# A hybrid encoder block on one core: the order of its first loads, of work at four seams, and of the last rows

## The chip, the cores and the metric

The kernel runs on one core of a Trainium2 chip. Its time is the device time of one execution in microseconds (us). Five engines work beside each other, each in the order of its own instruction list: PE (TensorE, matmuls and transposes), DVE (VectorE), ACT (ScalarE), POOL (GpSimd) and SP (SyncE, which here only issues DMAs). ACT and POOL can issue DMAs too. An instruction waits on semaphores for what it reads, and holds up what stands behind it on its engine.

## What is computed

x has 1024 rows of 1024 columns, fp32. Cut to what matters:

```
h      = rmsnorm(x) ; u = h @ w_in          # z, xbc, dt, s_b, s_c, s_x, g_a, g_b
y      = scan(silu(conv(xbc)), dt) * silu(z) # chunked state-space scan, 4 groups
y      = y * rsqrt(mean(y*y over a group)) * ssd_norm_w
branch_a = y @ w_ssd_proj
branch_b = (s_b * conv(s_c * s_x)) @ w_sconv_proj
x      = x + (sigmoid(g_a) * branch_a + sigmoid(g_b) * branch_b) @ w_o
f      = rmsnorm(x)
x      = x + (silu(f @ w_gate) * (f @ w_up)) @ w_down
out    = rmsnorm(x)
```

## The kernel before

**Matmuls.** Every large product is a Strassen-Winograd product of 2x2 blocks: seven block products in the order 1, 2, 6, 5, 7, 3, 4, on operands such as A11, S1 to S4 and B11, T1 to T4, which are sums of blocks. Each fp32 operand is split into a hi and a lo part (ACT writes hi: th, wh, wk, gh, qh; DVE subtracts for lo: tl, wl, wk, gl, ql), and each product of two tiles is three matmuls (`mmc`, L678 to L681: hi hi, lo hi, hi lo). A matmul of 128x512 starts some 0.23 us behind the one before it.

**Order.** The program is written out by hand: each engine runs its instructions in the order of the code. Generators (`put`, `step_norms`, `h1_rows`) are stepped from the loops of matmuls, so that a step's place in the loops is its place on DVE, ACT and POOL. Pages of 4 KB a partition are taken from a pool of 47 and go back when their readers are through.

**Prologue.** x lies in eight tiles of 128 rows (x0 to x7). SP issues x0 to x3 (L231), the first weight tile p0.y (`first[0].y.load()`, tile ws), x4 to x7 (`more_loads`, L245), p1.y and p2.y, the small weights of dt (wdts, L1501), and the three p.x. POOL issues six small loads of constants into c (L236 to L241), then d, dtbc and al. Rows 0 to 3 are squared by ACT, DVE, ACT, DVE (`rows_sq(..., "avav")`, L115 and L117). PE transposes the constants into pc (L1532, L1533), ACT copies them to cols (L1534). Then ACT's square root nr (L101) and four small DVE operations (L102 to L107) give the factors of the rows, rows are scaled (L135 on ACT, L137 on DVE), turned by PE (L1543), copied with the norm's weight (br), and split into th and tl.

**T2 seam.** `second_half` turns rows 4 to 7; a pass k of its loop writes one quarter of the raw blocks and of the sums t1 and t2 (L1602). `put("T1")` splits t1 in pass 3; `put("T2")` splits t2 behind the loop, one yield later. wk and u are parts of the weight operands and of the products' sums beside it.

**Norm seam.** The scan's output y is normed per group and half of the rows: gv, gr (L99 to L107) from the sums of squares pq, PE turns gr into prt (L532), ACT copies it to rst, POOL writes it to rs_d in memory (L536) and reads it back spread over all partitions (rbc, L538), DVE multiplies y by it (L543). When the second half of a group is done, its sums for the next product are made (L557) and written to yt_d (L558). Several norms run at once; `step_norms` steps them oldest first.

**h1 seam.** Before the FFN, the rows of the first half are scaled by their norm in `h1_rows(0, (2, 3))`: rows 2 and 3 on ACT (L135), the others on DVE (L137), turned, and split (gh, qh on ACT; gl, ql on DVE).

**Tail.** For each of the last four row tiles `fin` adds the two sums of squares (fss, L1423), takes the root (fr, L1411) and four small DVE operations, scales one half of the row on ACT (L1486) and one on DVE (L1428), and SP writes the row out (L1488).

Of the kernel before, what the change touches and what calls it, by code (L numbers as in the profile page):

```python
# [8 lines left out]
F32 = mybir.dt.float32  # L9
# [4 lines left out]
P = 128  # L14
# [25 lines left out]
def hybrid_block(ctx: ExitStack, tc: tile.TileContext, x, nmw, w_in, cw, cb, dtb, alog, dsk, snw,  # L40
# [15 lines left out]
    def nm(s):  # L56
        cnt[0] += 1
        return f"{s}_{cnt[0]}"
# [4 lines left out]
    def bank(s):  # L63
        return sm.tile([P, 512], F32, tag="sm", name=nm(s))
# [58 lines left out]
    def rows_sq(src, s, engs="aaaa"):  # L123
        acc = rows_acc(src, s)
        for e in engs:
            rows_sq_on(e, acc, s)
        return acc
# [29 lines left out]
    class Slab:  # L157
# [1 line left out]
            self.src, self.shape, self.s = src, shape, s  # L159
            self.st = self.hl = None  # L160

        def load(self):
            if self.st is None:
                self.st = page(self.s + "s", self.shape)
                nc.sync.dma_start(self.st, self.src)

        def split(self):
            if self.hl is None:
# [57 lines left out]
    xt = [page("x") for _ in range(NT)]  # L226
    wdt_s = sp.tile([P, KT * H], F32, tag="eb", bufs=3, name="wdts").rearrange("p (k h) -> p k h", h=H)
    warm = cp.tile([P, 1], F32, name="warm")
    nc.scalar.activation(warm, epst, AF.Sqrt)
    for i in range(4):  # L230
        nc.sync.dma_start(xt[i], x[i * P:(i + 1) * P, :])  # L231


    consts = page("c")
# [5 lines left out]
    nc.gpsimd.dma_start(rb[40:56, :], snw.rearrange("o (i p) -> (o i) p", p=P))  # L240
    nc.gpsimd.dma_start(rb[56:80, :], scw[0].rearrange("k (i p) -> (k i) p", p=P))  # L241

    def more_loads():
        for i in range(4, NT):
            nc.sync.dma_start(xt[i], x[i * P:(i + 1) * P, :])  # L245
    d2 = cp.tile([16, 2], F32, name="d2")

    dtbc = cp.tile([H, 1], F32, name="dtbc")
# [2 lines left out]
    def small_loads():  # L251
        nc.gpsimd.dma_start(d2, dsk.rearrange("o (i j) -> (o i) j", j=2))
        nc.gpsimd.dma_start(dtbc, dtb.rearrange("o h -> h o"))
        for q in range(4):
            nc.gpsimd.dma_start(al[32 * q:32 * q + 32, :], alog.rearrange("o h -> h o"))
# [305 lines left out]
    def scans():  # L561


        def step_norms():
            for n in list(norms):
                if next(n, 0) == 0:
                    norms.remove(n)

        def one(f, j):
            f(j)  # L570
            step_norms()

        want(0, 0)
        want(0, 2)
        prep(0)
        prep(1)
        prep_eb(1)
        yield
        prep2(0)
        for j in range(len(items)):  # L580
            one(part1, j)
            yield
            if j > 0:
                one(part2, j - 1)
                yield
        one(part2, len(items) - 1)
        yield
        while norms:
            step_norms()
            yield  # L590
# [553 lines left out]
    def h1_rows(half, act):  # L1144
        ts = range(4 * half, 4 * half + 4)
        s = sp.tile([P, 4], F32, tag="ssq", name=nm("hss"))
        V.tensor_add(s.unsqueeze(2), sq1[:, 4 * half:4 * half + 4, 0:1], sq1[:, 4 * half:4 * half + 4, 1:2])
        rows = rows_scale([h1[t] for t in ts], [hn[t] for t in ts], s, act=act)
        for t in ts:
            nc.sync.dma_start(h1_d[t], h1[t])  # L1150
            h1[t] = hn[t] = None
        return rows
# [10 lines left out]
    def ffn_phase():  # L1163
# [17 lines left out]
        raw0, raw1 = ([], []), ([], [])  # L1181

        def first_half():
            rows0 = h1_rows(0, (2, 3))
            yield
            yield
            yield from fill(rows0, raw0, 0, wcol)
            yield from put("B11", raw0[0])
            yield from put("B21", raw0[1])
# [214 lines left out]
            no = slice(j * 512, j * 512 + 512)  # L1404
            nc.scalar.activation(fo[t][:, no], h1[t][:, no], AF.Square, accum_out=sq[:, t, j:j + 1])

        def rstd2_of(ssq, n, s):

            shp = list(ssq.shape)
            r = sp.tile(shp, F32, tag="rr", name=nm(s + "r"))  # L1410
            nc.scalar.activation(r, ssq, AF.Sqrt, scale=1.0 / n, bias=epst)  # L1411
            v = sp.tile(shp, F32, tag="rv", name=nm(s + "v"))
            V.tensor_scalar(v, ssq, 1.0 / n, EPS, op0=ALU.mult, op1=ALU.add)
            V.reciprocal(r, r)
            q = sp.tile(shp, F32, tag="rq", name=nm(s + "q"))
            V.tensor_mul(q, r, r)
            V.tensor_mul(q, q, v)
            V.scalar_tensor_tensor(r, q, -3.0, r, op0=ALU.add, op1=ALU.mult)
            return r

        def finish(ms):
            s = sp.tile([P, len(ms), 1], F32, tag="fss", name=nm("fss"))
            V.tensor_add(s, sq[:, ms[0]:ms[-1] + 1, 0:1], sq[:, ms[0]:ms[-1] + 1, 1:2])  # L1423
            return rstd2_of(s.rearrange("p a b -> p (a b)"), D, "f")

        def out_rows(t, r, n):
            no = slice(n * 512, n * 512 + 512)
# [52 lines left out]
        tail = ds.chunks[ds.at:]  # L1480
        ds.ahead(len(ds.chunks), len(ds.chunks))

        def fin(m):
            t = 4 + m
            r = finish(range(t, t + 1))
            nc.scalar.activation(fo[t][:, 512:1024], h1[t][:, 512:1024], AF.Copy, scale=r)  # L1486
            out_rows(t, r, 0)
            nc.sync.dma_start(out[t * P:(t + 1) * P, :], fo[t])  # L1488

        for m in range(4):  # L1490
            for c in tail:
# [3 lines left out]


    first[0].y.load()
    more_loads()
    for p in first[1:]:
        p.y.load()  # L1500
    nc.sync.dma_start(wdt_s, w_in[:, DT0:DT0 + H].rearrange("(k p) f -> p k f", p=P))  # L1501
    for p in first:
        p.x.load()
    small_loads()
    loaded[0] = NF
    steps_ps, wdt_hl = [], []

# [17 lines left out]
            mmc(steps_ps[hf][:H], wh[:, kw, :], wl[:, kw, :], bh, bl, j == 0 and part == 0,  # L1525
                j == len(todo) - 1 and part == 1)

    a0 = rows_sq(xt[0:4], "x", "avav")
    a1 = rows_acc(xt[4:8], "x")
    del xt  # L1530
    pc = bank("pc")
    nc.tensor.transpose(pc[:, 0:96], ra, ident[:96, :96])  # L1532
    nc.tensor.transpose(pc[:, 96:176], rb, ident[:80, :80])  # L1533
    nc.scalar.activation(cols[:, 0:176], pc[:, 0:176], AF.Copy)  # L1534
    del consts, ra, rb
    r0 = rows_scale(*a0, act=(3,), parts=2)
    raw0, raw1 = ([], []), ([], [])
    turned = {}
# [53 lines left out]
    def second_half():  # L1592
        t1, t2 = [[page("t1", HB) for _ in range(2)] for _ in range(2)]
        for k in range(KT):
            if k % 2 == 0:
                raw1[k // 4].append(page("br", HB))
            turn_rows(r1, k)
            pt = turned.pop(k)
            o = k % 4 // 2, k % 2
            nc.scalar.activation(raw1[k // 4][o[0]][:, o[1], :], pt, AF.Copy, scale=nmc[:, k:k + 1])  # L1600
            less = (raw0[0] if k < 4 else t1)[o[0]][:, o[1], :]
            V.scalar_tensor_tensor((t1, t2)[k // 4][o[0]][:, o[1], :], pt, nmc[:, k:k + 1], less,  # L1602
                                   op0=ALU.mult, op1=ALU.subtract)
            if k == 3:
                raw0[0].clear()
                for j in range(2):
                    nc.sync.dma_start(b12_d[j], raw1[0][j])
                every(put("T1", t1))
            yield
        every(put("T2", t2))  # L1610
        yield
        every(put("B22", raw1[1]))
        yield
        for k in range(2):
            V.tensor_sub(raw1[0][k], raw1[1][k], raw1[0][k])
        every(put("T3", raw1[0]))
        raw1[0].clear()
        raw1[1].clear()
        yield
        for k in range(2):  # L1620
            V.tensor_sub(raw0[1][k], raw0[1][k], t2[k])
        every(put("T4", raw0[1]))
        raw0[1].clear()
        yield
# [104 lines left out]
```

## Time and profile before

| | |
|---|---|
| median of 3 runs | 1910.57 us (1910.33 to 1910.74) |
| profiled execution | 1910.68 us, its span 1908.9 us |
| PE busy | 1879.7 us, 98% of the span |
| DVE, ACT, POOL busy | 68%, 51%, 9% |
| DMA moved | 411.97 MB, mean 216 GB/s |
| chain that ended last | PE 92%, DVE 4%, ACT 2%, DMA 1%, issue 1% |

The span goes from the first to the last instruction of the profile. In rows of the timeline, the idle time ahead of an instruction and what ended it stand in brackets; idle time of PE is what a change here can give back.

### The profile page before, as it was taken

How to read it: one execution, taken by the hardware profiler on the slowest of the kernel's cores; microseconds unless marked ns; L12 is line 12 of the kernel's file. 1: busy time of each engine (PE TensorE's matmuls, PEld its weight loads, DVE VectorE, ACT ScalarE, POOL GpSimd, SP SyncE). 2: the span in 40 equal slices, each digit the busy share in tenths (PEclk: the TensorE clock that was granted, in tenths of full speed). 3: DMA queues.
4: the chain of work that ended last, by engine and by line, in shares of the span. 5: the costliest groups of instructions: out<-in, count | busy, mean ns of one | idle time of the engine just before them, and what ended most of it. 6: DMA issues, size and time to landing. Idle time of an engine off the chain costs nothing.

```text
span 1908.9 us, 24143 instructions
## 1 busy us (share of the span) xinstructions
PE 1879.7 (98%) x8905; PEld 1545.3 (81%) x8905; DVE 1299.4 (68%) x1688; ACT 970.6 (51%) x1541; POOL 169.7 (9%) x196
## 2 busy tenths in 40 slices
PE   7999999999999999999999999999999999999998
PEld 5688888888888888888878888887888888888886
DVE  7667878777785678889878548877444444456465
ACT  5545454444444987877665454464333333345333
POOL 1010111101100000101010000101211121100000
PEclk9999999999999999999999999999999999999999
DMA  5197999978959656778798665917988888867552
GB/s 181 48 275 173 240 230 236 240 187 226 264 149 288 223 194 219 251 250 269 261 321 311 226 208 203 229 80 171 215 193 220 195 193 192 232 257 286 190 196 110
DMA packets 341190, 411.97 MB, mean 216 GB/s; under 512 B 17384, under 2 KB 223936, under 8 KB 341072
## 3 DMA queue, kind: packets, MB, share of 16 engines
q1 hardware_dynamic: 284400, 308.59, 50.0%
q0 software_dynamic: 48608, 72.47, 20.9%
q10 hardware_dynamic: 8064, 29.36, 3.8%
q8 instruction: 70, 1.15, 0.2%
q14 instruction: 48, 0.39, 0.1%
HBM read 320.56 MB, written 143.15 MB: 243 GB/s over the span
## 4 chain that ended last, share of the span: by engine, by line
PE 92%; DVE 4%; ACT 2%; DMA 1%; issue 1%; SPq 0%; ACTq 0%; DVEq 0%
PE pb L679 5%; PE pb L680 5%; PE pb L681 5%; PE gb L679 5%; PE gb L680 5%; PE gb L681 5%; PE fb L681 4%; PE fb L679 4%; PE fb L680 4%; PE pr L81 4%; PE pr L83 4%; PE pr L82 4%; PE gd L679 4%; PE pd L679 4%; PE gd L681 4%; PE gd L680 4%
## 5 line engine op out<-in xcount | busy, mean ns | idle before, releaser
L77 DVE TENSOR_TENSOR wl<-ws,wh 128x1024 fp32r<-128x1024 f32 x77 | 94.0, 1221 | 121.6 <-ACT wh L76 121.6
L679 PE MATMUL gb<-qh,gh 128*128 128x512 f32 x432 | 169.1, 391 | 1.1 <-DVE h L1132 1.1
L680 PE MATMUL gb<-ql,gh 128*128 128x512 f32 x432 | 168.9, 391 | 0.0
L681 PE MATMUL gb<-qh,gl 128*128 128x512 f32 x432 | 168.7, 391 | 0.0
L681 PE MATMUL fb<-th,wl 128*128 128x512 f32 x352 | 137.1, 389 | 0.8 <-DVE wl L77 0.8
L679 PE MATMUL fb<-th,wh 128*128 128x512 f32 x352 | 137.1, 390 | 0.6 <-ACT wh L76 0.6
L680 PE MATMUL fb<-tl,wh 128*128 128x512 f32 x352 | 137.0, 389 | 0.0
L81 PE MATMUL pr<-th,wh 128*128 128x512 f32 x320 | 131.1, 410 | 0.0
L679 PE MATMUL gd<-qh,gh 128*128 128x512 f32 x324 | 126.0, 389 | 0.0
L680 PE MATMUL gd<-ql,gh 128*128 128x512 f32 x324 | 126.0, 389 | 0.0
L681 PE MATMUL gd<-qh,gl 128*128 128x512 f32 x324 | 126.0, 389 | 0.0
L83 PE MATMUL pr<-th,wl 128*128 128x512 f32 x320 | 125.1, 391 | 0.0
L82 PE MATMUL pr<-tl,wh 128*128 128x512 f32 x320 | 124.9, 390 | 0.0
L76 ACT ACTIVATE qh<-cb 128x1024 fp32r<-128x1024 f32 x98 | 99.8, 1018 | 38.0 <-PE gb L680 17.1
L77 DVE TENSOR_TENSOR ql<-cb,qh 128x1024 fp32r<-128x1024 f32 x98 | 115.6, 1180 | 1.6 <-ACT qh L76 1.4
L74 DVE SCALAR_TENSOR_TENSOR gl<-ca,gh 128x1024 fp32r<-128x1024 f32 (+1 forms) x60 | 70.5, 1174 | 49.0 <-ACT gh L73 49.0
L681 PE MATMUL fd<-th,wl 128*128 128x512 f32 x264 | 102.7, 389 | 0.0
L679 PE MATMUL fd<-th,wh 128*128 128x512 f32 x264 | 102.7, 389 | 0.0
L680 PE MATMUL fd<-tl,wh 128*128 128x512 f32 x264 | 102.7, 389 | 0.0
L679 PEld LDWEIGHTS gb<-qh,gh 128*128 128x128 f32 x432 | 81.5, 189 | 18.4 <-DVE h L1132 1.4
L679 PE MATMUL pb<-th,wh 128*128 128x512 f32 x240 | 94.4, 394 | 1.0 <-ACT u L894 1.0
L681 PEld LDWEIGHTS gb<-qh,gl 128*128 128x128 f32 x432 | 81.5, 189 | 17.1
(324 smaller groups left out, 4702.3 us busy)
## 6 DMA issues: line engine op xcount, KB each, us to landing
ws<-in_w_in_dram SPq DMA_DIRECT2D x80, 512.0 KB, 6.3
ws<-in_w_gate_dram SPq DMA_DIRECT2D x77, 256.0 KB, 3.9
ws<-in_w_up_dram SPq DMA_DIRECT2D x77, 256.0 KB, 4.4
ca<-u_d SPq DMA_DIRECT2D x35, 512.0 KB, 5.3
ab<-ac_d SPq DMA_DIRECT2D x32, 512.0 KB, 6.0
xbc_g<-cv ACTq DMA_DIRECT2D x24, 512.0 KB, 7.0
ws<-ws POOLq DMA_DIRECT2D x22, 512.0 KB, 6.4
wd_d<-in_w_down_dram SPq DMA_DIRECT2D x20, 512.0 KB, 10.8
```

Source lines behind the costliest of these rows:

```text
L74: nc.vector.scalar_tensor_tensor(lo, src, -1.0, hi.bitcast(F32), op0=ALU.mult, op1=ALU.subtract)
L76: nc.scalar.activation(hi, src, AF.Copy)
L77: nc.vector.tensor_sub(lo, src, hi.bitcast(F32))
L81: nc.tensor.matmul(o, lh, rh, start=first, stop=False)
L82: nc.tensor.matmul(o, lh, rl, start=False, stop=False)
L83: nc.tensor.matmul(o, ll, rh, start=False, stop=last)
L679: nc.tensor.matmul(o, lh, rh, start=first, stop=False, skip_group_check=True)
L680: nc.tensor.matmul(o, lh, rl, start=False, stop=False, skip_group_check=True)
L681: nc.tensor.matmul(o, ll, rh, start=False, stop=last, skip_group_check=True)
```

## The change

Five edits. (1) Loads of the prologue: x0 and x2 are issued by SP, x1 and x3 by ACT; SP then issues p0.y and nothing more. ACT issues x4 and x5 behind its square of x0, and x6, x7, p1.y and wdts behind its square of x2, and p2.y between cols and the root nr. POOL issues the three p.x behind the constants and ahead of d, dtbc and al. (2) `put("T2")` stands inside the last pass of the loop. (3) `step_norms` steps the newest norm first. (4) `h1_rows(0, (3,))`: row 2 is scaled by DVE. (5) In the tail the sum of squares of the first half of a row, known earlier, goes in as the bias of the root (one operation for the four rows, `known`), and the last row is written in two halves by ACT and SP.

```diff
+    for i in range(4):
+        (nc.scalar if i % 2 else nc.sync).dma_start(xt[i], x[i * P:(i + 1) * P, :])
     nc.scalar.activation(warm, epst, AF.Sqrt)
-    for i in range(4):
-        nc.sync.dma_start(xt[i], x[i * P:(i + 1) * P, :])
...
-    def more_loads():
-        for i in range(4, NT):
-            nc.sync.dma_start(xt[i], x[i * P:(i + 1) * P, :])
+    def more_loads(i):
+        for i in (i, i + 1):
+            nc.scalar.dma_start(xt[i], x[i * P:(i + 1) * P, :])
...
-            for n in list(norms):
+            for n in norms[::-1]:
...
-            rows0 = h1_rows(0, (2, 3))
+            rows0 = h1_rows(0, (3,))
...
+            r = sp.tile(shp, F32, tag="rr", name=nm("fr"))
+            nc.scalar.activation(r, ssq, AF.Sqrt, scale=1.0 / D, bias=b)
+            v = sp.tile(shp, F32, tag="fv", name=nm("fv"))
+            V.tensor_scalar(v, ssq, 1.0 / D, b, op0=ALU.mult, op1=ALU.add)
...
+        known = sp.tile([P, 4], F32, tag="rv", name=nm("fk"))
+        V.tensor_scalar(known.unsqueeze(2), sq[:, 4:8, 1:2], 1.0 / D, EPS, op0=ALU.mult, op1=ALU.add)
...
-            r = finish(range(t, t + 1))
+            r = rstd2_of(sq[:, t, 0:1], known[:, m:m + 1])
             nc.scalar.activation(fo[t][:, 512:1024], h1[t][:, 512:1024], AF.Copy, scale=r)
             out_rows(t, r, 0)
-            nc.sync.dma_start(out[t * P:(t + 1) * P, :], fo[t])
+            if m < 3:
+                nc.sync.dma_start(out[t * P:(t + 1) * P, :], fo[t])
+            else:
+                nc.scalar.dma_start(out[t * P:(t + 1) * P, 512:1024], fo[t][:, 512:1024])
+                nc.sync.dma_start(out[t * P:(t + 1) * P, 0:512], fo[t][:, 0:512])
...
-    more_loads()
-    for p in first[1:]:
-        p.y.load()
-    nc.sync.dma_start(wdt_s, w_in[:, DT0:DT0 + H].rearrange("(k p) f -> p k f", p=P))
-    for p in first:
-        p.x.load()
-    small_loads()
...
-    a0 = rows_sq(xt[0:4], "x", "avav")
+    a0 = rows_acc(xt[0:4], "x")
+    rows_sq_on("a", a0, "x")
+    more_loads(4)
+    rows_sq_on("v", a0, "x")
+    rows_sq_on("a", a0, "x")
+    more_loads(6)
+    first[1].y.load(nc.scalar)
+    nc.scalar.dma_start(wdt_s, w_in[:, DT0:DT0 + H].rearrange("(k p) f -> p k f", p=P))
+    rows_sq_on("v", a0, "x")
     a1 = rows_acc(xt[4:8], "x")
     del xt
+    for p in first:
+        p.x.load(nc.gpsimd)
+    small_loads()
...
     nc.scalar.activation(cols[:, 0:176], pc[:, 0:176], AF.Copy)
     del consts, ra, rb
+    first[2].y.load(nc.scalar)
...
-            yield
-        every(put("T2", t2))
+            if k == 7:
+                every(put("T2", t2))
+            yield
```

ACT's list at the start of the program, before (x_85 to x_88 are rows 0 to 3, ws_182 is p0.y):

```order
L229 ACT_TABLE_LOAD
L229 ACTIVATE warm<-epst 128x1
L117 ACTIVATE xn_206,xss_205<-x_85 128x1024
L117 ACTIVATE xn_210,xss_205<-x_87 128x1024
L1534 ACTIVATE cols<-pc_215 128x176
L101 ACTIVATE nr_221<-nv_219 128x4
```

The same place of the changed kernel (x_89 to x_92 are rows 4 to 7, ws_195 is p1.y, ws_217 is p2.y):

```order
L117 ACTIVATE xn_185,xss_184<-x_85 128x1024
L245 DMA x_89<-in_x_dram 128x1024
L245 DMA x_90<-in_x_dram 128x1024
L117 ACTIVATE xn_191,xss_184<-x_87 128x1024
L245 DMA x_91<-in_x_dram 128x1024
L245 DMA x_92<-in_x_dram 128x1024
L165 DMA ws_195<-in_w_in_dram 128x8x128
L1537 DMA wdts<-in_w_in_dram 128x8x32
L1547 ACTIVATE cols<-pc_213 128x176
L165 DMA ws_217<-in_w_in_dram 128x8x128
L101 ACTIVATE nr_221<-nv_219 128x4
```

Between the squares and the root nr stand seven DMA issues now, the last of them behind cols.

DVE's list at the T2 seam, before (t_72 and t_73 are the two halves of T2, s_93 and s_100 weight sums):

```order
L1602 SCALAR_TENSOR_TENSOR t_73_425<-pt_558,cols,t_71_423 128x512
L868 TENSOR_TENSOR wk_548<-s_93_546,wk_548 128x512
L847 TENSOR_TENSOR s_100_581<-ws_195,ws_188 128x512
L77 TENSOR_TENSOR tl_586<-t_72_424,th_585 128x1024
L77 TENSOR_TENSOR tl_590<-t_73_425,th_589 128x1024
L868 TENSOR_TENSOR wk_583<-s_100_581,wk_583 128x512
```

The same place of the changed kernel (s_104 is the sum that was s_100):

```order
L1616 SCALAR_TENSOR_TENSOR t_73_425<-pt_558,cols,t_71_423 128x512
L77 TENSOR_TENSOR tl_566<-t_72_424,th_565 128x1024
L77 TENSOR_TENSOR tl_570<-t_73_425,th_569 128x1024
L869 TENSOR_TENSOR wk_548<-s_93_546,wk_548 128x512
L848 TENSOR_TENSOR s_104_589<-ws_203,ws_195 128x512
```

The two tl stand ahead of the first wk and the next sum now.

DVE's list at the last norm, before (y_7211 and y_7212 are rows of the norm before it):

```order
L543 SCALAR_TENSOR_TENSOR y_7211<-y_7211,cols,rbc_8235 128x512 x2
L543 SCALAR_TENSOR_TENSOR y_7212<-y_7212,cols,rbc_8235 128x512 x2
L99 TENSOR_SCALAR gv_8383<-pq_8378 128x4
L102 RECIPROCAL gr_8385<-gr_8385 128x4
L104 TENSOR_TENSOR gq_8388<-gr_8385 128x4
L105 TENSOR_TENSOR gq_8388<-gq_8388,gv_8383 128x4
L106 TENSOR_SCALAR gq_8388<-gq_8388 128x4
L107 TENSOR_TENSOR gr_8385<-gr_8385,gq_8388 128x4
```

The same place of the changed kernel:

```order
L544 SCALAR_TENSOR_TENSOR y_7211<-y_7211,cols,rbc_8233 128x512 x2
L99 TENSOR_SCALAR gv_8380<-pq_8375 128x4
L102 RECIPROCAL gr_8382<-gr_8382 128x4
L104 TENSOR_TENSOR gq_8385<-gr_8382 128x4
L105 TENSOR_TENSOR gq_8385<-gq_8385,gv_8380 128x4
L106 TENSOR_SCALAR gq_8385<-gq_8385 128x4
L107 TENSOR_TENSOR gr_8382<-gr_8382,gq_8385 128x4
L544 SCALAR_TENSOR_TENSOR y_7212<-y_7212,cols,rbc_8233 128x512 x2
```

The whole chain from gv to gr stands ahead of the second pair of rows now. On POOL, where the order was yt_d T3, rs_d, rbc, yt_d T4, it is rs_d, rbc, yt_d T3, yt_d T4.

## Rows read from the trace of the kernel before

**Rows 1.** The page, busy time of each engine, its share and instructions:
```profile
PE 1879.7 (98%) x8905; PEld 1545.3 (81%) x8905; DVE 1299.4 (68%) x1688; ACT 970.6 (51%) x1541; POOL 169.7 (9%) x196
```

**Rows 2.** Timeline (start, length in us), prologue: ACT's, then one of DVE:
```profile
8.41 1.06 ACT L117 ACTIVATE xn<-x 128x1024 f32<-128x1024 f32 x1 [3.16 <-DMA x<-in_x_dram]
...
10.70 0.32 ACT L1534 ACTIVATE cols<-pc 128x176 f32<-128x176 f32 x1 [1.14 <-PE pc L1533]
11.41 0.20 ACT L101 ACTIVATE nr<-nv 128x4 f32<-128x4 f32 x1 [0.39 <-DVE nv L99]
...
13.90 1.04 ACT L864 ACTIVATE wh<-ws 128x1024 fp32r<-128x1024 f32 x1
...
9.86 1.23 DVE L115 SCALAR_TENSOR_TENSOR xn<-x 128x1024 f32<-128x1024 f32 x1 [3.13 <-DMA x<-in_x_dram]
```

**Rows 3.** Timeline of PE in the prologue:
```profile
10.30 0.36 PE L1533 MATMUL pc<-ident,c 80*128 80x80 f32 x1 [1.88 <-DMA c<-in_sconv_w_dram]
...
20.41 0.50 PE L680 MATMUL pb<-tl,wh 128*128 128x512 f32 x1 [0.61 <-DVE tl L77]
```

**Rows 4.** Timeline of SP's DMA issues in the prologue (the length is that of the issues):
```profile
2.60 0.44 SPq L165 DMA_DIRECT2D ws<-in_w_in_dram  x1
...
7.59 5.51 SPq L165 DMA_DIRECT2D ws<-in_w_in_dram  x2
13.15 3.15 SPq L1501 DMA_DIRECT2D wdts<-in_w_in_dram  x1
```

**Rows 5.** Issues later: ACT's, SP's (timeline); DMA view from 100.2 us (KB, us to landing):
```profile
514.41 0.33 ACTq L606 DMA_DIRECT2D xbc_g<-cv  x1
...
471.12 14.58 SPq L165 DMA_DIRECT2D ws<-in_w_in_dram  x1
...
ws<-in_w_in_dram SPq DMA_DIRECT2D x1, 512.0 KB, 16.8
```

**Rows 6.** Timeline at the T2 seam: DVE, ACT, PE:
```profile
53.19 1.41 DVE L1602 SCALAR_TENSOR_TENSOR t<-pt,cols,t 128x512 f32<-128x512 f32 x2 [1.34 <-ACT br L1600]
...
53.73 0.60 ACT L897 ACTIVATE u<-pd 128x512 f32<-128x512 f32 x1
...
57.46 0.49 PE L679 MATMUL pb<-th,wk 128*128 128x512 f32 x1 [0.45 <-ACT th L76]
58.72 0.50 PE L680 MATMUL pb<-tl,wk 128*128 128x512 f32 x1 [0.77 <-DVE tl L77]
59.06 0.40 PE L681 MATMUL pb<-th,wk 128*128 128x512 f32 x1
```

**Rows 7.** Timeline of PE, a later product:
```profile
75.79 0.50 PE L680 MATMUL pb<-tl,wh 128*128 128x512 f32 x1 [0.27 <-DVE tl L77]
```

**Rows 8.** Timeline at the last norm: DVE, PE, POOL:
```profile
979.12 2.74 DVE L543 SCALAR_TENSOR_TENSOR y<-y,cols,rbc 128x512 f32<-128x512 f32 x4 [2.89 <-DMA rbc<-rs_d]
...
983.22 0.27 PE L532 MATMUL prt<-ident,gr 128*4 128x128 f32 x1 [2.12 <-DVE gr L107]
...
964.32 0.72 POOL L558 DMA_DIRECT2D yt_d<-y  x1 [2.69 <-DVE y L557]
...
972.20 0.57 POOL L538 DMA_DIRECT2D rbc<-rs_d  x1 [6.64 <-PE gd L681]
```

**Rows 9.** Stretches: length, busy PE, PEld, DVE, ACT, POOL; granted clock; DMA share, GB/s:
```profile
984.00:988.00 4.00, 4.00 (x12) 3.11 (x11) 4.00 (x5) 2.70 (x6) 0.53 (x1) 0.57 0.93 272
...
1253.40:1256.00 2.60, 1.47 (x7) 1.19 (x7) 2.60 (x5) 1.42 (x5) 0.00 (x0) 1.00 0.00 0
```

**Rows 10.** Timeline at the start of the FFN: ACT, PE:
```profile
1248.41 2.19 ACT L135 ACTIVATE hn<-h,nr 128x1024 f32<-128x1024 f32 x2 [1.10 <-DVE nr L107]
...
1254.60 0.50 PE L679 MATMUL gb<-qh,gh 128*128 128x512 f32 x1 [1.13 <-DVE h L1132]
```

**Rows 11.** Timeline of the tail: ACT's last root, DVE's last rows:
```profile
1903.44 0.29 ACT L1411 ACTIVATE fr<-fss,epst 128x1 f32<-128x1 f32 x1 [0.23 <-DVE fss L1423]
...
1904.55 0.75 DVE L1428 SCALAR_TENSOR_TENSOR fo<-h,fr,fb 128x512 f32<-128x512 f32 x1
```

More of the change, by code (lines that the diff above doesn't have):

```diff
@@ L160, in __init__, with load @@
             self.st = self.hl = None
-        def load(self):
+        def load(self, eng=None):
             if self.st is None:
                 self.st = page(self.s + "s", self.shape)
-                nc.sync.dma_start(self.st, self.src)
+                (eng or nc.sync).dma_start(self.st, self.src)
         def split(self):
@@ L1405, in squares, with rstd2_of @@
             nc.scalar.activation(fo[t][:, no], h1[t][:, no], AF.Square, accum_out=sq[:, t, j:j + 1])
-        def rstd2_of(ssq, n, s):
+        def rstd2_of(ssq, b):
             shp = list(ssq.shape)
[L1410 to L1413, printed above, removed]
+            r = sp.tile(shp, F32, tag="rr", name=nm("fr"))
+            nc.scalar.activation(r, ssq, AF.Sqrt, scale=1.0 / D, bias=b)
+            v = sp.tile(shp, F32, tag="fv", name=nm("fv"))
+            V.tensor_scalar(v, ssq, 1.0 / D, b, op0=ALU.mult, op1=ALU.add)
             V.reciprocal(r, r)
-            q = sp.tile(shp, F32, tag="rq", name=nm(s + "q"))
+            q = sp.tile(shp, F32, tag="rq", name=nm("fq"))
             V.tensor_mul(q, r, r)
@@ L1423, in finish @@
             V.tensor_add(s, sq[:, ms[0]:ms[-1] + 1, 0:1], sq[:, ms[0]:ms[-1] + 1, 1:2])
-            return rstd2_of(s.rearrange("p a b -> p (a b)"), D, "f")
+            return rstd2_of(s.rearrange("p a b -> p (a b)"), epst)
         def out_rows(t, r, n):
```

## Prediction

> **What bounds the kernel now.** I read the page's busy shares first: PE runs matmuls for 98% of the span [rows 1], so a change is worth what it does to the places where PE stands still. I then read the timeline of PE for rows with idle time ahead of them, and for each the engine named as releaser. Four such places are touched by the change: the prologue, where the second matmul starts at 20.41 us [rows 3]; the T2 seam near 58 us [rows 6]; the last group norm near 982 us [rows 8]; the start of the FFN near 1254 us [rows 10]. The fifth is the tail behind the last matmul [rows 11]. Everything is summed against the profiled run's own 1910.7 us (span 1908.9), which is the median of the runs within 0.1 us.
>
> **Prologue: the only part with two answers.** The chain is: x rows land, two engines square them, a square root nr on ACT, the scaling of the rows, 32 transposes, hi and lo splits, matmuls. The root starts at 11.41 behind cols at 10.70, which follows the transposes of the constants, and these wait at 10.30 for GpSimd's last constant load [rows 2, 3]. The last of the four rows is squared by DVE from 9.86 on, for 1.23 us [rows 2]. So two things reach ACT at nearly the same time: the constants (cols over at 11.0) and the row statistics (11.2).
> The change loads the four rows alone. The last may land some 1 to 2 us earlier than 9.8. This takes away only one of the two waits: the constants still go through GpSimd, and cols stays ahead of the root in ACT's order. By the row, cols ends at 10.70+0.32 = 11.02.
> The new cost is on ACT. Besides two x rows at the very start it now issues seven loads ahead of the root: two behind its first square, four behind its second (8.41+1.06+0.19 = 9.6 before), and one, the second-next weight tile, between cols and the root. An issue of ACT that finds room takes 0.33 us [rows 5], so the four fit between the second square and cols (9.6 + 4 x 0.33 = 10.9, a few tenths late at worst), and the last puts the root at 11.02+0.33 = 11.35 to 11.7: against 11.41 that is **about +0.3, or nothing**. Does it find room? In before's SP queue the third weight load and the small wdts load did not: two weight issues take 5.51 us together (the first, like the one at 2.60, some 0.4), wdts 3.15 us [rows 4]. Ahead of the last of ACT's loads stand, per DMA engine, four rows of 8 packets, a weight tile of 64 and wdts of 64, less what has gone: over 100, and SP stood still with 118 to 168 ahead by my count of its issues and their sizes. So ACT, which is now in the critical chain where SP never was, may stand still for 3.15 us (the wdts row, which is the nearest: same kind of queue, similar load) up to 4.7 (5.51 less 0.4 and the 0.4 gap). The root then starts at 11.02+3.15 = 14.2 or 15.7, **+2.8 to +4.3**, and nothing behind it has slack: nr, six scalings, transposes, th and tl follow each other. Against this a gain: should the constants come earlier, with less traffic beside them, at most -0.5 (the root cannot start before the four issues are over at 10.9).
> Also the first weight tile p0.y, issued at 2.60 before [rows 4] and at about 1.7 after, shares the DMA engines with ACT's and GpSimd's loads once the rows are through. Before, ACT's split of it at 13.90 did not wait [rows 2]. The worst price in the trace for such a load, issued while another queue moved rows, is 16.8 us [rows 5]: it would land at 18.5 and hold that split by 4.6. Its bounds are so 0 and +4.6; I take 0, near the row of this very load, since its 64 small packets per engine can start as soon as SP's two rows are through, before ACT's next rows are issued.
> The Trainium skill, DMA: Bandwidth & Descriptors, section Queues, rings and completion order, speaks against this: each DMA engine takes turns between the queues that have work, packet by packet, so that a queue of small packets falls behind beside one of large ones. The 16.8 us agree with it; that the split at 13.90 did not wait says nothing, since SP's queue was alone then. By that rule the case without a stop ends up to 4.6 later, by the row of this load not at all.
> I take the stop, at its lower row: **+2.8**.
>
> **T2 seam.** PE waits 0.45 for ACT's th at 57.46 and 0.77 for DVE's tl at 58.72 [rows 6]. With T2 put a turn earlier, ACT splits th from about 53.7 on (where u<-pd stood), DVE's tl follows its t rows (53.19+1.41 = 54.6) to some 57.1. Behind them the lo part of wk, which stood ahead of them, now ends near 57.7, and the third matmul wants it at 57.3: the third matmul, at 59.06 before (two rows of 0.23 behind the wait), is then at 57.7, 1.2 to 1.3 us earlier. A part is given back at 75.79, where PE waits 0.27 for another tl [rows 7] and DVE has gained less than PE. **-0.8** (-0.4 to -1.2).
>
> **Norm seam.** At 981.1 PE reaches prt, which needs gr, and waits 2.12 us [rows 8]. DVE, idle for 2.89 until rbc lands, first does four rows of L543 (2.74 us), and only then the norm's chain, 1.36 us to PE's start, which reads none of them. After, the chain goes behind two of them: 1.37 earlier. And rs_d goes to GpSimd's queue ahead of T3's 512 KB yt_d write, which before was issued at 964.32, just in front [rows 8]; rs_d to rbc should land about 1 us sooner. Together 2.3 us: gr is ready at about 980.8, before PE asks. Behind the gap the trace has a granted clock of 0.57 for four microseconds, that is partly the lower of the two levels, 1.2 instead of 2.4 GHz [rows 9]: 4 x 0.43 = 1.7 us lost. The clock stayed full around the gap of 1.13 at 1254 [rows 9, 10], so with no gap or a short one this goes too. 2.1+1.7 = 3.8, less 0.2 for a rest: **-3.6** (-2.6 to -3.9). If only DVE's order helps and the clock still falls: -1.3. The price is that T3's write lands some 7 us later (it stands behind rbc, which waits for rs_d; rbc is at 972.20 before); its readers are loads that run several chunks ahead, so I cost it at nothing, 0 to 0.5. The other norms' chains are ahead of their sums already without a wait of PE, and I cost those at nothing.
>
> **h1 seam.** PE waits 1.13 at 1254.60 for h, which comes from ACT's gh and qh through DVE; ACT is held by two scalings of 2.19 us together [rows 10]. One goes to DVE, which waits for that gh itself: 1.1 earlier. **-1.1** (-0.9 to -1.3).
>
> **Tail.** The sum fss (0.16 us and its gap) leaves the path twice: in the last row, where fr starts at 1903.44 instead of behind ACT's accumulator, and in the row before it, which lets the last h start earlier. 0.2 each. The output in halves moves the same bytes and starts with both halves ready at 1905.3, as now. **-0.4** (-0.2 to -0.6). The one extra small operation on DVE lies beside matmuls.
>
> **The sum.** -0.8 - 3.6 - 1.1 - 0.4 = -5.9 (-4.1 to -6.8), and the prologue +2.8: 1910.7 - 5.9 + 2.8 = **1907.6**.
>
> **Rivals.**
> A, no stop. ACT's queue is its own and was never full, and its issues took 0.33 where SP's stood still near by (at 471 one of SP's took 14.58 [rows 5]). Then the prologue is +0.4 at most: 1910.7 - 5.9 + 0.3 = 1905.1 (1903.6 to 1906.7). What speaks for it is that room is by queue; against it that this queue would hold as much as SP's did when it stopped.
> B, the norm seam gives only 1.3, since rbc's trip (6.9 us) is not shortened or the clock falls all the same: with the stop 1909.9.
> C, slower. The stop is one of the long kind: with p0.y and GpSimd's x tiles taking turns with ACT's rows, the queue empties at a half or a third of the pace that SP's had alone. The issue at 471.12 that took 14.58 us [rows 5] is the longest that the trace shows: the root would start at 25.6, +14.2, and the kernel would take 1919. It decides from a stop of about 10 us on (5.9 + 3.8). For it speaks that three queues are busy there; against it that no stop in the prologue of before was over 4.7, with more bytes in one queue. 1914.5 to 1919.
> D, no stop, but p0.y late by that 4.6 between the other queues: 1905.1 + 4.6 - 0.3 = 1909.4, for and against as told above.
> That the change does not do what it says: the changes at the seams leave PE's order of products as it was, only DVE's, ACT's and GpSimd's orders move, and a seam could find its next wait a few tenths later. This is in the bounds of the terms.
>
> **Chances.** The stop 0.46, A 0.36, B 0.06, C 0.07, D 0.05. About 0.2% (3.8 us) is what a measurement can tell from no change: 1906.8 and 1914.4. Faster: all of A (0.36) and of the stop the part with its short end (0.07): 0.43. Slower: C, 0.07. Within: the rest, 0.50. The range runs from the better part of A to beyond B: 1903.8 to 1911.0; the stop alone has 1906.2 to 1909.6.
>
> **What would show it.** In the profile after: the length of ACT's issue between cols and nr (0.3 or over 3 us) and the start of nr; the second matmul at 20.4 to 20.8 or 22.8 to 24.7; PE's waits at T2 near 57 below 0.6; prt without a wait over 0.5 and the clock near 1.00 behind it; PE's first gb of the FFN without a wait; the last output about 0.4 nearer to the last matmul. The prediction is wrong if the root starts before 11 us, if gr still comes after PE asks, or if a load that reads yt_d holds PE.

## The result and the profile after

The changed kernel takes 1913.77 us (median of 19 runs, 1912.89 to 1914.39), the kernel before 1908.77 in as many runs beside it (1907.55 to 1910.75): a ratio of 1.0023, interval 1.0017 to 1.003. It is slower, by 0.2%. The forecast was 1907.6 in a range of 1903.8 to 1911.0, 3.1 us under the kernel before and no change that can be told from none; it came 5.0 us over it, outside the range and the other way. The kernel before runs in two groups, 10 of these 19 runs at 1907.55 to 1908.77 and 9 at 1910.07 to 1910.75, and 1910.68, the execution from whose profile the forecast was summed, is of the longer group, which by the runs beside the experiments has a mean granted clock of 0.998 against 0.999.

The changed kernel's profile (span 1912.4) shows what was expected of the three seams, and a prologue that costs nearly three times the forecast. ACT's timeline of the changed kernel in the prologue (start and length in us; rows of ACTq are issues of DMAs):

```profile
9.09 0.55 ACTq L165 DMA_DIRECT2D ws<-in_w_in_dram  x1
...
9.66 5.25 ACTq L1537 DMA_DIRECT2D wdts<-in_w_in_dram  x1
14.96 0.32 ACT L1547 ACTIVATE cols<-pc 128x176 f32<-128x176 f32 x1 [5.60 <-issue]
14.99 3.92 ACTq L165 DMA_DIRECT2D ws<-in_w_in_dram  x1
18.96 0.21 ACT L101 ACTIVATE nr<-nv 128x4 f32<-128x4 f32 x1 [3.68 <-issue]
```

The issue of wdts takes 5.25 us and that of p2.y 3.92, on the engine that is to take the root: cols starts at 14.96 where [rows 2] has 10.70, nr at 18.96 instead of 11.41. What both wait for was long there, as PE's timeline shows:

```profile
9.35 0.36 PE L1546 MATMUL pc<-ident,c 80*128 80x80 f32 x1 [0.97 <-DMA c<-in_sconv_w_dram]
...
20.84 1.45 PE L1557 MATMUL pt<-ident,xn 128*128 128x128 f32 x4 [11.13 <-DVE xn L137]
...
27.96 0.50 PE L681 MATMUL pb<-tl,wh 128*128 128x512 f32 x1
```

The constants came a microsecond sooner than in [rows 3], the rows were squared by 9.8, and PE then stood for 11.13 us. Its second matmul is at 27.96 instead of 20.41: +7.55.

PE's list is the same in both kernels, so the difference of the starts of one and the same matmul tells what each stretch gave or took. Against the profile that the prediction used (starts in us; the last row goes to the end of the span):

| stretch, by PE's time before | difference of starts | given (-) or taken (+) | forecast |
|---|---|---|---|
| prologue, to 20.41 | 0 to +7.55 | +7.55 | +2.8 |
| T2 seam, to 75.79 | to +6.89 | -0.66 | -0.8 |
| two waits for u at 189.59 and 477.10 | to +6.32 | -0.57 | none |
| near 834 to 843 | to +8.15 | +1.83 | 0 to +0.5 |
| last norm, the wait | to +5.90 | -2.25 | -1.9 |
| behind it, the clock | to +4.28 | -1.62 | -1.7 |
| to the FFN, small | to +4.43 | +0.15 | none |
| h1 seam | to +3.44 | -0.99 | -1.1 |
| tail | to +3.47 | +0.03 | -0.4 |

The rows of the seams, PE's timeline of the changed kernel:

```profile
65.29 0.50 PE L682 MATMUL pb<-th,wk 128*128 128x512 f32 x1 [0.27 <-DVE wk L869]
...
82.67 0.50 PE L681 MATMUL pb<-tl,wh 128*128 128x512 f32 x1 [0.76 <-DVE tl L77]
...
842.54 0.50 PE L83 MATMUL pr<-th,wl 128*128 128x512 f32 x1 [1.51 <-DVE wl L991]
...
989.12 0.27 PE L533 MATMUL prt<-ident,gr 128*4 128x128 f32 x1
...
1258.04 0.50 PE L680 MATMUL gb<-qh,gh 128*128 128x512 f32 x1
```

The two waits of [rows 6] are gone and the third matmul waits 0.27 for the lo part of wk; half of it is given back where [rows 7] has 0.27 and this has 0.76. prt, PE's turn of gr, no longer waits (2.12 in [rows 8]); the first matmul of the FFN has no wait (1.13 in [rows 10]). New is a wait of 1.51 us at 842.54, for a wl that stands in a late DVE list. DVE's timeline has its source 20 us earlier, and POOL's shows the writes that it names:

```profile
822.39 0.69 DVE L438 TENSOR_TENSOR xx<-pxt,wdt 128x512 f32<-128x512 f32 x1 [6.06 <-DMA yt_d<-y]
...
812.62 0.59 POOL L539 DMA_DIRECT2D rbc<-rs_d  x1 [5.86 <-DMA ws<-in_w_in_dram]
813.21 1.44 POOL L559 DMA_DIRECT2D yt_d<-y  x2
```

DVE stands 6.06 us until the page under xx is free, and that page's last reader is a write to yt_d that POOL now issues behind rbc, T3's and T4's both from 813.21 on. From 822.39 to the wl that PE waits for DVE idles for no more than 0.27 us at a time.

### The profile page after: what moved, and what is told of

It reads as the page before. It is cut to its first block, busy times and chain, and to the rows that moved or that the text cites. A ratio compares the mean times of both kernels' runs of the same rounds, so it can differ in the third digit from the quotient of the medians.

```text
span 1912.4 us, 24142 instructions
## 1 busy us (share of the span) xinstructions
PE 1878.7 (98%) x8905; PEld 1544.3 (81%) x8905; DVE 1299.8 (68%) x1686; ACT 968.5 (51%) x1540; POOL 172.8 (9%) x199
## 4 chain that ended last, share of the span: by engine, by line
PE 92%; DVE 4%; ACT 2%; DMA 1%; issue 1%; ACTq 1%; SPq 0%; DVEq 0%
PE pb L680 5%; PE pb L681 5%; PE pb L682 5%; PE gb L680 5%; PE gb L681 5%; PE gb L682 5%; PE fb L682 4%; PE fb L680 4%; PE fb L681 4%; PE pr L81 4%; PE pd L680 4%; PE pd L682 4%; PE pd L681 4%; PE pr L83 4%; PE pr L82 4%; PE gd L681 3%
## 5 line engine op out<-in xcount | busy, mean ns | idle before, releaser
L681 PEld LDWEIGHTS gb<-ql,gh 128*128 128x128 f32 x432 | 81.1, 188 | 17.0 <-DVE ql L77 0.4
```

Source lines behind the costliest of these rows:

```text
L681: nc.tensor.matmul(o, lh, rl, start=False, stop=False, skip_group_check=True)
```

## The experiments

Two theories stood at first: that the loss is the prologue's, and that the seams lose as well.

**The seams with before's prologue** (all its loads on SP again, in their old order; cuts are marked with ...):

```diff
-        (nc.scalar if i % 2 else nc.sync).dma_start(xt[i], x[i * P:(i + 1) * P, :])
...
+        nc.sync.dma_start(xt[i], x[i * P:(i + 1) * P, :])
...
+    for i in range(4, NT):
+        nc.sync.dma_start(xt[i], x[i * P:(i + 1) * P, :])
+    for p in first[1:]:
+        p.y.load()
+    nc.sync.dma_start(wdt_s, w_in[:, DT0:DT0 + H].rearrange("(k p) f -> p k f", p=P))
+    for p in first:
+        p.x.load()
...
-    more_loads(4)
...
-    more_loads(6)
-    first[1].y.load(nc.scalar)
-    nc.scalar.dma_start(wdt_s, w_in[:, DT0:DT0 + H].rearrange("(k p) f -> p k f", p=P))
...
-        p.x.load(nc.gpsimd)
...
-    first[2].y.load(nc.scalar)
```

> The change with the prologue of before put back (all of SP's loads in their old order); the four seams and the tail as in the change. Theory 1 (the loss lies in the prologue alone, the seams give what their waits cost): second matmul at 20.4 us as before; from there on PE's starts as in the changed kernel less 7.55 us, so 3.4 - 7.55 = -4.1 us against before in the profile, 1906.6 against its 1910.7, and the median 2 to 4 us under before's. Theory 2 (the seams as such lose, with the later stall of 1.67 us near 842 as their sign): within 1 us of before.

1905.42 us (1904.91 to 1906.08) beside 1908.66: ratio 0.9982, interval 0.9973 to 0.9992. So the three seams and the tail are worth 3.2 us, the later stall included (PE waits 1.19 us there), and the first theory holds. Its prologue is that of before, but not its times: nr is at 10.00 instead of 11.41, and then ACT waits for wdts. ACT's timeline of this kernel:

```profile
10.00 0.21 ACT L101 ACTIVATE nr<-nv 128x4 f32<-128x4 f32 x1 [0.22 <-DVE nv L99]
...
19.83 0.42 ACT L1522 ACTIVATE wdt<-wdts 128x256 fp32r<-128x256 f32 x1 [2.17 <-DMA wdts<-in_w_in_dram]
```

**The prologue alone, on before.**

> Before with the changed prologue alone. Theory 1: wdts' issue on ACT about 5.2 us, p2.y's 3.9, root nr at 19.0, second matmul at 28.0, the whole 7.5 us over before. Theory 2 (the prologue's loss is given back later by loads that are ahead): under 4 us over before.

1918.97 us in one run, 10.3 over a median of 1908.66 and 8.3 over the 1910.68 of the first profile, which has the same fall of the clock behind the last norm. wdts' issue took 5.28 us and p2.y's 3.93, nr was at 19.24, and PE's starts are 7.83 us behind those of the first profile from the first transposes of the rows on, 7.5 to 7.8 later and 7.76 at the end. Next to nothing is given back. The two parts account for the whole: about +8 and -3.

**What stops ACT.** Theory R: the room in ACT's own queue. Rival S: the DMA engines shared by three queues. First, ACT issues x rows only:

```diff
+    for p in first[1:]:
+        p.y.load()
+    nc.sync.dma_start(wdt_s, w_in[:, DT0:DT0 + H].rearrange("(k p) f -> p k f", p=P))
...
-    first[1].y.load(nc.scalar)
-    nc.scalar.dma_start(wdt_s, w_in[:, DT0:DT0 + H].rearrange("(k p) f -> p k f", p=P))
...
-    first[2].y.load(nc.scalar)
```

> The change, but p1.y, wdts and p2.y are issued by SP behind p0.y; ACT issues x rows only, GpSimd still the three p.x. Theory R (ACT stops because its own queue holds only some 145 packets per DMA engine): no issue of ACT over 0.6 us, cols at 9.8, root nr at 10.1 to 10.4; p0.y, 13.2 us on its way in the change, then decides: ACT's split of it starts at 14.9 or later, second matmul at 20.5 to 22. Rival S (the stop comes from three queues that share the DMA engines, whoever issues): ACT's issues of rows or cols late as well, root after 13.

1909.37 us in one run. ACT's timeline:

```profile
10.22 0.21 ACT L101 ACTIVATE nr<-nv 128x4 f32<-128x4 f32 x1
...
16.48 1.06 ACT L865 ACTIVATE wh<-ws 128x1024 fp32r<-128x1024 f32 x1 [3.68 <-DMA ws<-in_w_in_dram]
```

ACT's stop is gone with the two weight loads and wdts, though from 9 to 15 us ACT's and GpSimd's queues were about as busy (46.6% and 44.4% of the engines' time, 50.0% and 46.6% in the change): against S. The stops went with the loads to SP, which stood 10.73 us over its three weight issues and 5.84 over wdts, and computes nothing. The root is at 10.22, and the next wait shows at once: the split of p0.y stands 3.68 us until that tile lands, and the second matmul is at 20.95.

Second, GpSimd's three loads on SP, with ACT's list untouched:

```diff
-        p.x.load(nc.gpsimd)
+        p.x.load()
```

> The change, but the three p.x are issued by SP behind p0.y instead of by GpSimd; ACT's list is that of the change. Theory R: ACT still stops, since 95 packets per engine of its own and wdts' 64 do not fit, only for less long, as its rows move without a third queue beside them: root nr at 14 to 17 instead of 19.0. Rival S: no stop, root before 11.

```profile
9.79 1.65 ACTq L1537 DMA_DIRECT2D wdts<-in_w_in_dram  x1
11.49 0.32 ACT L1547 ACTIVATE cols<-pc 128x176 f32<-128x176 f32 x1 [2.09 <-issue]
12.53 3.96 ACTq L165 DMA_DIRECT2D ws<-in_w_in_dram  x1
16.54 0.20 ACT L101 ACTIVATE nr<-nv 128x4 f32<-128x4 f32 x1 [4.73 <-issue]
```

1911.23 us in one run. ACT stops all the same, for 1.65 and 3.96 us; wdts' stop is shorter by 3.6 and p2.y's as long as in the change. Who has to wait is set by what stands in ACT's own queue, how long in part by the company: without GpSimd's tiles ACT's queue had 78.4% of the engines' time from 9 to 15 us instead of 50.0%. S is part of the size and not the cause.

Third and fourth, how much room. wdts on SP; then wdts, x6 and x7 on SP:

```diff
     first[0].y.load()
+    nc.sync.dma_start(wdt_s, w_in[:, DT0:DT0 + H].rearrange("(k p) f -> p k f", p=P))
...
-    nc.scalar.dma_start(wdt_s, w_in[:, DT0:DT0 + H].rearrange("(k p) f -> p k f", p=P))
```

> The change, but wdts is issued by SP behind p0.y, so ACT has only p1.y and, behind cols, p2.y of small packets. Theory R with room for some 145 packets per engine: cols goes at 9.8, p2.y (32 of rows, 64 of p1.y, 64 of its own = 160) waits until some 15 are gone, which at half a DMA engine's pace is near 15 us: root at 14 to 16. Rival (wdts' 128-byte packets, or the third load in the queue as such, made the stop): p2.y's issue under 0.6 us, root before 11.

```profile
10.36 5.13 ACTq L165 DMA_DIRECT2D ws<-in_w_in_dram  x1
15.54 0.21 ACT L101 ACTIVATE nr<-nv 128x4 f32<-128x4 f32 x1 [4.87 <-issue]
```

The place of wdts is taken by p2.y: 5.13 us (1910.57 us in one run). It is not wdts' rows of 128 bytes that stop an issue, but what stands ahead.

```diff
     first[0].y.load()
+    for i in (6, 7):
+        nc.sync.dma_start(xt[i], x[i * P:(i + 1) * P, :])
+    nc.sync.dma_start(wdt_s, w_in[:, DT0:DT0 + H].rearrange("(k p) f -> p k f", p=P))
...
-    more_loads(6)
...
-    nc.scalar.dma_start(wdt_s, w_in[:, DT0:DT0 + H].rearrange("(k p) f -> p k f", p=P))
```

> The change, but x6, x7 and wdts are issued by SP behind p0.y; ACT keeps x4, x5, p1.y and, behind cols, p2.y. Theory R with room for some 145 packets per engine: ahead of p2.y stand at most 16 packets of rows, of which several are gone by 10 us, and 64 of p1.y, so with its own 64 it fits: issue under 0.6 us, root nr at 10.4 to 11.2 instead of 15.5 with x6 and x7 on ACT. Rival (a second load of small packets in one queue stops whatever stands ahead): issue over 2 us, root after 13. PE's second matmul is then set by p0.y's landing beside three queues, near 20 to 22.

```profile
10.13 2.72 ACTq L165 DMA_DIRECT2D ws<-in_w_in_dram  x1
12.89 0.21 ACT L101 ACTIVATE nr<-nv 128x4 f32<-128x4 f32 x1 [2.45 <-issue]
```

1907.61 us in one run. R's number missed: by the count of packets issued and ended in the trace, 77 per engine were ahead of p2.y and 64 are its own, 141, so by R it should have fitted, and it stood 2.72 us. The rival, that a second load of small packets stops, expected an issue over 2 us, which came, and a root after 13, which came at 12.89. SP's queue in this trace speaks against a count of packets as well; SP's timeline:

```profile
2.13 3.42 SPq L1508 DMA_DIRECT2D x<-in_x_dram  x2
5.59 0.53 SPq L1509 DMA_DIRECT2D wdts<-in_w_in_dram  x1
```

x6 and x7, 8 packets per engine each, stood 3.42 us together behind p0.y with 80 ahead; wdts, 64 packets, went in 0.53 behind x7 with 85 ahead. In the eight traces in which ACT issues more than x1 and x3, each stop of ACT came right behind a load of 64 small packets per engine (p1.y or wdts), and none of its other issues, rows or p1.y behind rows, took over 0.65. So it is shown that ACT stops by what stands in its own queue; room by a count of packets, R's reason, is not shown, and whether the load right ahead does it by itself was not tried. The packets left when a stop ended do not settle on a number either: 135 to 145 per engine behind p1.y, 166 to 178 behind wdts.

**The stall at 842.** The change, with the newest norm first from the seventh norm on only, so that T3's writes go out ahead of rs_d at the norms before:

```diff
-    halves, norms, kept = {}, [], {}
+    halves, norms, kept, seen = {}, [], {}, []
...
+            seen.append(g)
...
-            for n in norms[::-1]:
+            for n in (norms[::-1] if len(seen) > 6 else list(norms)):
```

> The change, with the newest norm first only from the seventh norm on, so that three T3 writes go out ahead of rs_d as before; prologue as in the change (second matmul at 28.0). Theory P: DVE's xx does not wait 6 us for yt_d near 816, PE's wait of 1.5 us at 842 is gone, and PE's starts behind it are 1.7 to 1.8 us earlier than in the change; span 1910.6. Rival (the wait comes from the late prologue, which shifts loads against each other): the wait stays.

POOL's timeline of this kernel, then DVE's:

```profile
805.07 0.72 POOL L560 DMA_DIRECT2D yt_d<-y  x1 [2.22 <-DVE y L559]
...
814.34 0.72 POOL L560 DMA_DIRECT2D yt_d<-y  x1
...
816.62 0.69 DVE L438 TENSOR_TENSOR xx<-pxt,wdt 128x512 f32<-128x512 f32 x1 [0.18 <-PE pxt L427]
```

1912.39 us in one run. T3's write goes out at 805.07, 8.1 us earlier than in the change, and xx waits 0.18 us instead of 6.06, with the late prologue untouched (and with before's prologue PE still had a wait here, 1.19 us). PE's wait at 842 is gone; its starts are 1.54 us earlier there, 1.7 soon behind it, and the span is 1910.4 instead of 1912.4. So the stall comes from T3's write behind rbc (theory P): the order of norms cost 1.5 to 1.8 us at one norm to win at another.

**The tail.** The changed kernel with the last row written whole:

```diff
-            if m < 3:
-                nc.sync.dma_start(out[t * P:(t + 1) * P, :], fo[t])
-            else:
-                nc.scalar.dma_start(out[t * P:(t + 1) * P, 512:1024], fo[t][:, 512:1024])
-                nc.sync.dma_start(out[t * P:(t + 1) * P, 0:512], fo[t][:, 0:512])
+            nc.sync.dma_start(out[t * P:(t + 1) * P, :], fo[t])
```

> The change with the last row written whole by SP. From the last matmul's start to the end of the span: before 7.70, changed kernel 7.72, both candidates with a whole row 7.37 and 7.37. If halves cost: 7.4 here. If the tail of the changed kernel was a scatter of its own: 7.4 too in other runs with halves (the run with seams alone has 7.37), and nothing can be said.

1913.88 us in one run. From the last matmul's start to the span's end it has 7.59 us. Over all profiles: without fss and with a whole row 7.37 or 7.38 (the three candidates below) and 7.59; with halves 7.72, 7.71, 7.71, 7.70, 7.71, 7.44 and 7.37; with before's tail 7.70, 7.70 and 7.91. One and the same tail differs by 0.2 to 0.35 us from profile to profile. So the shorter chain seems worth up to 0.33 us, and halves seem to take most of it back; neither is shown, since this run lies between.

**Candidates.** The change with only x1 and x3 of the prologue on ACT; T3 first and the last row whole, by the edits above:

```diff
     for i in range(4):
         (nc.scalar if i % 2 else nc.sync).dma_start(xt[i], x[i * P:(i + 1) * P, :])
...
     first[0].y.load()
+    for i in range(4, NT):
+        nc.sync.dma_start(xt[i], x[i * P:(i + 1) * P, :])
+    for p in first[1:]:
+        p.y.load()
+    nc.sync.dma_start(wdt_s, w_in[:, DT0:DT0 + H].rearrange("(k p) f -> p k f", p=P))
+    for p in first:
+        p.x.load()
...
-    more_loads(4)
...
-    more_loads(6)
-    first[1].y.load(nc.scalar)
-    nc.scalar.dma_start(wdt_s, w_in[:, DT0:DT0 + H].rearrange("(k p) f -> p k f", p=P))
...
-        p.x.load(nc.gpsimd)
...
-    first[2].y.load(nc.scalar)
```

> The seams of the change with three edits: of the prologue only x1 and x3 on ACT's queue are kept (all other loads on SP in before's order); the newest norm goes first only from the seventh norm on, so that the earlier T3 writes go out ahead of rs_d again; the last row goes out whole. Theory P (the stall of 1.67 us near 842 comes from T3's write queued behind rbc): no stall of PE over 0.5 us near 835, the wait at the last norm gone as in the change. Theory Q (it comes from DVE's norm chain standing ahead of wl): since the order at that norm is that of before it also goes, but then DVE's tile xx would not wait for the yt_d write in the change; its row there tells. Root nr at 10.0 to 10.4; second matmul near 18.7; from 34 us on the gain shrinks to 0.6, since ACT waits for wdts (2.2 us in the run with before's prologue). Median 5 to 6 us under before.

1904.12 us beside 1908.97: ratio 0.9978, interval 0.9969 to 0.9988. That is 4.9 us, just under the 5 to 6 expected; its runs reach from 1904.01 to 1906.14. Root at 10.33, second matmul at 19.33, no wait at 842. ACT waits 1.32 us for wdts, as foreseen, if shorter. The next one issues wdts ahead of p1.y and p2.y:

```diff
+    nc.sync.dma_start(wdt_s, w_in[:, DT0:DT0 + H].rearrange("(k p) f -> p k f", p=P))
     for p in first[1:]:
         p.y.load()
-    nc.sync.dma_start(wdt_s, w_in[:, DT0:DT0 + H].rearrange("(k p) f -> p k f", p=P))
```

> As c1, with wdts issued ahead of p1.y and p2.y. If wdts' landing is what held ACT (2.2 us at 19.8 in the run with before's prologue), its split starts without a wait near 17.7, the second half of the rows is normed 1 to 1.5 us earlier, and the kernel takes about 1 us less than c1. If the second half is held by another load or by DVE, it is level with c1.

```profile
10.35 0.20 ACT L101 ACTIVATE nr<-nv 128x4 f32<-128x4 f32 x1
...
18.07 0.40 ACT L1519 ACTIVATE wdt<-wdts 128x256 fp32r<-128x256 f32 x1
```

1903.78 us beside 1908.97: ratio 0.9974, interval 0.9964 to 0.9983. The wait for wdts is gone, but the gain over the first candidate is 0.3 us and not 1: the intervals overlap. And with all four rows on SP's queue again (behind `warm`, ACT's first activation, as before):

```diff
-        (nc.scalar if i % 2 else nc.sync).dma_start(xt[i], x[i * P:(i + 1) * P, :])
+        nc.sync.dma_start(xt[i], x[i * P:(i + 1) * P, :])
```

> As c2, but all four first rows on SP's queue, as before: what is left of the change's prologue is only wdts ahead of p1.y and p2.y. If two queues bring the rows sooner: root nr later than c2's 10.35 by up to 1 us, kernel 0.3 to 0.7 us slower than c2's ratio of 0.9974. If one queue is as fast where it doesn't pause (root at 10.0 in the run with before's prologue): level with c2 within 0.3 us, with some runs slower where the queue pauses near 5 us.

1903.66 us (1903.12 to 1904.06) beside 1908.42: ratio 0.9971, interval 0.996 to 0.9982. It is level with the two queues, though its profile has the pause, 217 GB/s from 5 to 6 us, and the root at 11.21: stretches (length, busy PE, PEld, DVE, ACT, POOL; granted clock; DMA share, GB/s) of this kernel:

```profile
5.00:6.00 1.00, 0.00 (x0) 0.00 (x0) 0.41 (x1) 0.33 (x2) 1.00 (x3) 1.00 0.71 217
```

So two queues for the first rows are worth nothing that these runs can measure. All three candidates are faster than the kernel before, by 0.2 to 0.3%, and so than the changed one; the last is the simplest.

**Before, a second time.**

> The kernel before, for a second profile. Its runs lie in two groups, about 1908.3 and 1910.5. If the DMA pause at 5 to 6 us of the first profile (178 GB/s) makes the difference, this one shows x2's square earlier than 8.41 when the run is of the lower group, and the same clock behind 983 us. If the clock's fall behind the wait at 983 makes it, a run of the lower group shows a full clock there.

1908.02 us. Its stretches, and PE's timeline at the last norm:

```profile
5.00:6.00 1.00, 0.00 (x0) 0.00 (x0) 0.46 (x1) 0.39 (x2) 1.00 (x3) 1.00 1.02 379
...
983.00:988.00 5.00, 5.00 (x23) 4.13 (x22) 5.00 (x6) 3.68 (x8) 0.53 (x1) 1.00 0.94 320
...
982.23 0.27 PE L532 MATMUL prt<-ident,gr 128*4 128x128 f32 x1 [1.36 <-DVE gr L107]
```

Both things are there. The pause near 5 us is missing and the second matmul 0.7 us earlier, of which 0.3 is left by 40 us; the wait at the norm is 1.36 us instead of 2.12 (rbc landed sooner: DVE waits 2.12 us for it instead of the 2.89 of [rows 8]), and behind it the clock stayed at 1.00, where [rows 9] has 0.57. These 0.3, 0.8 and the clock's 1.6 make up the 2.7 us between the two profiles' spans. Against this profile the changed kernel's prologue costs 8.25 us, and the last norm gives 1.5, wait and clock together, and not 3.9: 6.1 in all between these two executions (1908.02 and 1914.39), against the 5.0 of the medians.

## Why the prediction was wrong, point by point

**The prologue's stop: right in kind, short by a whole stop, and this decided.** The prediction named the place and the engine: an issue on ACT ahead of the root that stands still and holds the root. The step that failed is that the four issues behind the second square find room, wdts among them: it gave wdts 0.33 us, and wdts stood 5.25, with 93 packets per engine ahead. The one stop that it did price, p2.y's, came as priced: 3.92 us, between its 3.15 and 4.7, in part by luck, since with wdts on SP it was 5.13. The two together put nr at 18.96, against 10.22 with the three loads taken off ACT, and PE's second matmul at +7.55 where the sum has +2.8. The trace of before had a sign of it beside the rows that the prediction read, in SP's timeline:

```profile
0.74 1.82 SPq L231 DMA_DIRECT2D x<-in_x_dram  x4
...
3.08 4.46 SPq L245 DMA_DIRECT2D x<-in_x_dram  x4
```

Four issues of rows took 1.82 us ahead of p0.y and 4.46 behind it, with some 90 packets ahead. The prediction counted packets and took over 118 as what stops an issue; neither this row nor p2.y's 2.72 us with 77 ahead fits such a count.

The company is the rest of the size. The price came from a queue that ran alone; here ACT's queue had half of the engines' time. The DMA view of the changed kernel from 9 to 15 us (ACT's queue is q10, GpSimd's q0, SP's q1; packets, MB, share):

```profile
q10 hardware_dynamic: 324, 1.20, 50.0%
q0 software_dynamic: 303, 1.11, 46.6%
q1 hardware_dynamic: 301, 0.15, 8.2%
```

ACT's rows and GpSimd's tiles share the engines packet for packet; with the tiles on SP wdts stood 1.65 us. The rival with a stop of the long kind had this part of the mechanism. The price that came, 7.55, lies between its 14.2 and the forecast's 2.8, and the time just below its 1914.5 to 1919. [rows 4] already has two stops behind one another, 4.7 and 3.15, so its chance of 0.07 was little.

**The sum.** By medians the seams and the tail gave 3.2 us (forecast 5.9) and the prologue took 8.2, the 5.0 of the whole and these 3.2 (forecast 2.8). Three smaller slips decide nothing: the strong ends of its seam terms add up to -7.0, not -6.8; the stop alone reaches 1910.9 with its upper price of 4.3, not 1909.6; and by [rows 6] the third matmul at T2 wants its operand at 57.47, not 57.3.

**p0.y beside other queues: taken at nothing, and hidden.** SP's queue moved 0.15 MB in those six microseconds, and p0.y landed 13.2 us after its issue. The Trainium skill, DMA: Bandwidth & Descriptors, section Queues, rings and completion order, says that the engines take turns between queues packet by packet; the trace agrees, 324, 303 and 301 packets from three queues, of which SP's are the small ones. In the changed kernel the root was later still, so it cost nothing there; with ACT's stop gone it cost 3.68 us of ACT's time. The prediction's upper bound, 4.6, was near, its choice of 0 was not. The reason given, that p0.y's packets start ahead of ACT's next rows, failed: ACT issued x4 at 5.45, and the first packet of p0.y came at 7.47, behind SP's rows.

**The gains of the seams: right for T2 and h1, at the last norm for the profiled execution alone.** T2 0.66 (forecast 0.8, with the lo part of wk as next wait and the part given back as worked out), h1 0.99 (1.1). At the last norm 2.25 and 1.62 (1.9 and 1.7) against the first profile, but 1.5 together against the second, whose wait was 1.36 us and whose clock did not fall. With DVE's old order the wait was 1.36, 2.12 and 2.29 us in three profiles: one execution is no price for a gap that hangs on a DMA's landing.

**T3's write: costed at nothing, and the reason failed.** The prediction gave the readers of yt_d, which run ahead, as the reason. What waited was not a reader of the data but the next owner of the page, xx on DVE, 6.06 us, and of this 1.5 to 1.8 came through to PE, three times the bound of 0.5.

**The tail: forecast 0.4, came 0.** With a whole row up to 0.33 us of it may be there, and the halves, taken as free, may cost about as much; the spread of the tails leaves both open.

**Not foreseen:** two waits of PE of 0.25 us for u are gone in the changed kernel (0.57 of starts). The first is gone in every other changed kernel too, the second in all but two of the candidates, and their cause was not tried.

## What to carry to other kernels

An engine that computes on the critical chain should not issue several loads of small packets ahead of that chain: here one such load behind rows went in 0.39 to 0.59 us, and the next stood 1.65 to 5.29. Look in the trace for every issue that stood still, rows too, and expect a stop to last longer when other queues are busy. When a DMA is moved back in a queue, look for who waits for the page that it reads, not only for its data. Price a gap that ends with a DMA's landing from several executions.

## What the runs showed of the chip that was not expected

- A DMA issue that stands holds its engine, arithmetic and all: 1.65, 2.72, 3.92, 3.96, 5.13, 5.25 us on ACT, each right behind a load of 64 small packets per engine in the same queue; its other issues there took 0.65 at most. A count of packets does not explain it: 77 ahead and 64 of its own stood 2.72 us on ACT, 85 and 64 went in 0.53 on SP.
- The clock behind PE's wait at the last norm: after 2.12 us it was granted 0.57 in the four microseconds of [rows 9]; after 2.29 us, with the changed prologue on before, it fell as well; after 1.36 us it was 1.00. The stretch of that second kernel:

```profile
992.00:998.00 6.00, 6.00 (x21) 4.71 (x21) 5.77 (x6) 3.58 (x6) 0.53 (x1) 0.72 0.96 322
```

- With the first four rows on one queue the DMA engines paused near 5 us in two of four profiles (178 and 217 GB/s against 379 and 397); on two queues in none of ten (385 to 437). What makes it pause is open.
